# Layer 0's mixing-gate modulation: partial sums on TensorE in four column groups instead of on VectorE

## The chip, the core and the metric

The kernel runs on one core of a Trainium2 chip. The metric is device time in microseconds (us) of one execution. Five engines work side by side, each on its own queue in order: PE (TensorE, the matrix unit; the profile lists its weight loads apart as PEld), DVE (VectorE), ACT (ScalarE), POOL (GpSimd) and SP (SyncE), which here issues all the DMAs. Tiles live in SBUF; matrix products land in PSUM, in banks of 512 fp32 columns on 128 partitions.

## What is computed

A two-layer decoder trunk on 256 tokens of width 2048, in fp32. Each layer first turns a conditioning vector c into six modulation vectors of 2048 numbers, by a product with a weight matrix of 2048 x 12288:

```python
c_act = jax.nn.silu(c)
for l in range(DEPTH):                                   # DEPTH = 2
    mod = (c_act @ w_mod[l] + b_mod[l])[:, None, :]
    shift_a, scale_a, gate_a, shift_m, scale_m, gate_m = jnp.split(mod, 6, axis=-1)
    h = modulate(rms_norm(x, g_pre_mix[l]), shift_a, scale_a)
    y = hybrid_mixer(h, positions, w_in[l], ...)         # MoBA, NSA and FoX heads, then @ w_out
    x = x + gate_a * rms_norm(y, g_post_mix[l])
    h = modulate(rms_norm(x, g_pre_mlp[l]), shift_m, scale_m)
    x = x + gate_m * rms_norm(sq_relu_mlp(h, w_up[l], w_down[l]), g_post_mlp[l])
```

The six vectors are called modulation groups 0 to 5. Group 2 is gate_a, the mixing gate. For layer 0 it is needed when the product with w_out[0] leaves PSUM.

## The kernel before

**The big products.** Every weight matrix is streamed from HBM in units of 512 rows x 512 columns (1 MB, tile `raw`, [128, 4, 512]). `unit` (L225) loads one, and for each half of it ACT rounds to fp32r (`hi`, L241) and DVE takes the rest (`lo`, L242). PE then multiplies with three fp32r products (L259 to L261, `gemm_b`) or two (L287 and L289, `chunk_a`). `raw` comes from a pool of four buffers (`rawp`), `hi` and `lo` from pools of four each, so about two units are converted ahead of PE.

**The modulation.** `mod_chunk` (L119) makes part of one group. It is a generator: at each `yield` one step of 1 MB of w_mod is done. Such a step is called by `tick` after a unit of a big product or a head of attention (a `Spread` sets how many steps go to how many ticks), so the steps lie between the units. The weights come into `rawm`, from the same four buffers as `raw`, or in turn into one larger buffer (`S3` in this stretch). The step has two forms:

- On DVE: the tile is [128, 2, 1024], and for each of its two slices DVE does acc += raw * cact, with cact a number for each partition (L149 for the first slice of a chunk, L151 for the others). A chunk of 1024 columns takes 8 steps.
- On PE (`pe=True`): the tile is [128, 4, 512]. Four matmuls, one for each slice, put cact, spread to 32 columns, against the slice; each writes 32 of the 128 partitions of one PSUM tile `pm`. ACT copies `pm` to acc in the first step of a chunk (L153), DVE adds it to acc in the others (L155). A chunk of 512 columns takes 4 steps.

```python
acc = wk.tile([128, w], F32, tag="acc" if w == 1024 else "bb", name="acc", bufs=1)   # L121
...
T.matmul(pm[32 * k:32 * k + 32], cs.to_broadcast([128, 32]), raw[:, k], start=True, stop=True,
         tile_position=(0, 32 * k))                                                  # L142
...
bb = wk.tile([128, 512], F32, tag="bb", name="bb", bufs=1)                           # L165
dma(bb, ...)                                                                         # L168, bias
dma(gb, ...)                                                                         # L169, gain
T.matmul(ps, ones, acc[:, i * 512:(i + 1) * 512], start=True, stop=True)             # L171
V.scalar_tensor_tensor(bb, ps, part, bb, op0=OP.mult, op1=OP.add)                    # L172
V.scalar_tensor_tensor(gg[:, ci:ci + 512], bb, D ** 0.5, gb, op0=OP.mult, op1=OP.mult)  # L173
```

At the end of a chunk the 128 partitions of acc are summed by a matmul with ones. For a gate this is L171, once for each 512 columns; DVE then adds the bias (L172) and multiplies by the gain (L173) into `gg`. Tiles with one tag share the tag's buffers: `acc` of a 512-column chunk and `bb` have the tag "bb", which has one buffer; `acc` of a 1024-column chunk has a buffer of its own.

PSUM tiles named `pst` (`ps_t`, L68) come from two banks. They serve `pm`, the sums of L171, and in the attention heads the transposes (L463, L721) and the outputs (`po`: L726, L469, L470). `pss` (scores, L439 to L445) has two banks, `psg` (big products) four.

**Where the group lies.** In layer 0 the generator `rest` runs groups 4, 2 and 3 in this order (`G0`, L33, L585). The forms on PE are used only for groups 1 and 0 at the start (`mod_first`, L565). In the profile, group 2's steps run from 336 to 424 us: first beside the NSA heads (L718 to L732) and the first four FoX heads (`fox_attn(0)`, L763), then beside `fox_group(1)` (L645), which makes q and k of the last four heads with eight weight units. A scheduler orders each engine's instructions within the dependencies, so that an engine's order is not just the order of the code.

Of the kernel before, what the change touches and what calls it, by code (L numbers as in the profile page):

```python
# [32 lines left out]
G0 = ((0, 4), (0, 2), (0, 3))  # L33
# [12 lines left out]
def trunk(ctx, tc, x, c, positions, w_mod, b_mod, g_pre_mix, g_post_mix, g_pre_mlp, g_post_mlp, w_in, b_forget,  # L46
# [137 lines left out]
                V.scalar_tensor_tensor(m, m, 1.0, gpre[l][g // 3][:, cols], op0=OP.add, op1=OP.mult)  # L184
        yield

    def mod_groups(*lg):
        for l, g in lg:
            for q in range(2):
                yield from mod_chunk(l, g, q, 1024)  # L190

    class Spread:
        def __init__(self, gen, units, over):
# [356 lines left out]
    for l in range(DEPTH):  # L550
# [3 lines left out]
        if l == 0:  # L554
# [14 lines left out]
            def rotate(q, c0, w, parts):  # L569
# [4 lines left out]
                for t in range(2):  # L574
                    s0 = 0
                    for dst in parts:
# [5 lines left out]
                        else:  # L582
                            V.tensor_tensor(d, pw, d, OP.add)

            rest = mod_groups(*G0)  # L585

            def mod_both(q):
                for i, _ in enumerate(mod_first(q)):
# [38 lines left out]
        else:  # L627
            h, act = nxt
            ring[0] = RA
            spread[0] = Spread(mod_groups(*G1), 32, R1)  # L630

        oT = [big(TS["o"][0], [128, 8, 2, 256])]
# [173 lines left out]
        if l == 0:  # L806
            spread[0] = Spread(mod_groups((1, 1), (1, 0), (1, 4), (0, 5)), 64, MA)
        else:
            spread[0] = Spread(mod_groups((1, 5)), 16, MB)
# [131 lines left out]
```

## Time and profile before

| | us |
|---|---|
| median of 3 runs | 2440.83 (2439.29 to 2443.04) |
| the profiled execution | 2435.61 |
| its span, first to last instruction | 2433.8 |
| PE busy in the span | 2364.5 (97%) |
| DVE busy | 1641.5 (67%) |
| ACT busy | 1202.5 (49%) |

In a row of a timeline stand the start, the duration, engine, line, operation, tiles and shapes, and in brackets the idle time just before, with what ended it. Matmuls are pipelined, so the time a matmul takes from PE is read from the start of one to the start of the next, not from its duration. An fp32 matmul appears as two instructions (x2 in a row).

### The profile page before, as it was taken

What the parts mean: (1) busy time and instruction counts of PE and PEld (TensorE: products, weight loads), DVE (VectorE), ACT (ScalarE), POOL (GpSimd) and SP (SyncE); (2) the same over time, 40 slices, a digit from 0 to 9 for tenths busy, and PEclk for the clock granted to TensorE, in tenths of its full rate; (3) what the DMA queues carried; (4) which work ended last, traced back from release to release, by engine and by line L of the source; (5) the groups of instructions that cost most, each with busy time, mean ns of one, the idle gap of its engine ahead of it and who ended that gap; (6) DMA issues with size and microseconds to landing.
All of it is one profiled execution on the core that took longest, in us unless ns stands there. A gap on an engine that the chain in (4) does not pass through costs nothing.

```text
span 2433.8 us, 31894 instructions
## 1 busy us (share of the span) xinstructions
PE 2364.5 (97%) x12396; PEld 1964.0 (81%) x12396; DVE 1641.5 (67%) x2247; ACT 1202.5 (49%) x2001; POOL 12.5 (1%) x20
## 2 busy tenths in 40 slices
PE   5999999999999999999999999999999999999998
PEld 2678778778888888888877879888888888888887
DVE  3458678878777777777568467765755665655555
ACT  3434444455545535535545455554654553553553
POOL 0000000000000000000000000000000000000000
PEclk8999999999999999999999999999999999999999
DMA  9788988988888888888657688865666667666653
GB/s 356 285 326 298 307 300 288 351 303 292 279 310 278 309 296 286 303 283 308 202 184 280 209 282 303 282 231 186 222 225 225 225 231 231 219 203 199 189 190 121
DMA packets 292120, 632.82 MB, mean 260 GB/s; under 512 B 10609, under 2 KB 44801, under 8 KB 291713
## 3 DMA queue, kind: packets, MB, share of 16 engines
q1 hardware_dynamic: 291968, 630.79, 75.5%
q8 instruction: 97, 1.59, 0.3%
q14 instruction: 55, 0.44, 0.0%
HBM read 628.65 MB, written 2.10 MB: 259 GB/s over the span
## 4 chain that ended last, share of the span: by engine, by line
PE 90%; DVE 4%; DMA 3%; ACT 1%; issue 1%; POOL 0%; SPq 0%; DVEq 0%; POOLq 0%; ACTq 0%
PE psg L287 16%; PE psg L260 15%; PE psg L259 15%; PE psg L261 15%; PE psg L289 8%; PE psu L287 6%; PE psu L289 3%; PE psr L260 2%; PE psr L259 2%; PE psr L261 1%; PE pst L142 1%; PE pst L180 1%; DMA raw<-in_w_in_dram 1%; DMA S<-in_w_mod_dram 1%; DVE lo L242 1%; PE pst L340 1%
## 5 line engine op out<-in xcount | busy, mean ns | idle before, releaser
L242 DVE TENSOR_TENSOR lo<-raw,hi 128x1024 fp32r<-128x1024 f32 (+2 forms) x768 | 908.3, 1190 | 540.4 <-ACT hi L241 539.1
L241 ACT CAST hi<-raw 128x1024 fp32r<-128x1024 f32 (+2 forms) x768 | 781.7, 1025 | 900.3 <-PE psg L261 444.1
L259 PE MATMUL psg<-hi,S 128*128 128x512 f32 (+2 forms) x1664 | 639.8, 386 | 2.3 <-DVE S L354 1.2
L287 PE MATMUL psg<-S,hi 128*128 128x512 f32 x1792 | 640.1, 398 | 1.5 <-DVE lu L437 0.6
L260 PE MATMUL psg<-lo,S 128*128 128x512 f32 (+2 forms) x1664 | 638.0, 383 | 2.0 <-DVE lo L242 2.0
L261 PE MATMUL psg<-hi,S 128*128 128x512 f32 (+2 forms) x1664 | 636.8, 383 | 0.9 <-DVE S L355 0.9
L289 PE MATMUL psg<-S,lo 128*128 128x256 f32 x1792 | 500.8, 281 | 0.9 <-DVE lo L242 0.9
L287 PEld LDWEIGHTS psg<-S,hi 128*128 128x128 f32 x1792 | 336.9, 188 | 83.1 <-ACT hi L241 2.0
L259 PEld LDWEIGHTS psg<-hi,S 128*128 128x128 f32 x1664 | 312.1, 188 | 68.1 <-issue 4.5
L260 PEld LDWEIGHTS psg<-lo,S 128*128 128x128 f32 x1664 | 312.8, 188 | 62.1 <-DVE lo L242 3.6
L261 PEld LDWEIGHTS psg<-hi,S 128*128 128x128 f32 x1664 | 312.6, 188 | 61.4 <-DVE S L355 2.6
L289 PEld LDWEIGHTS psg<-S,lo 128*128 128x128 f32 x1792 | 338.3, 189 | 3.6 <-DVE lo L242 1.8
L151 DVE SCALAR_TENSOR_TENSOR acc<-rawm,cact,acc 128x1024 f32<-128x1024 f32 x226 | 289.3, 1280 | 26.6 <-DMA rawm<-in_w_mod_dram 24.9
L287 PE MATMUL psu<-S,hi 128*128 128x512 f32 x640 | 232.9, 398 | 0.0
L289 PE MATMUL psu<-S,lo 128*128 128x256 f32 x640 | 179.0, 280 | 0.0
L287 PEld LDWEIGHTS psu<-S,hi 128*128 128x128 f32 x640 | 120.2, 188 | 29.4 <-DVE xu L840 0.3
L289 PEld LDWEIGHTS psu<-S,lo 128*128 128x128 f32 x640 | 120.7, 189 | 0.3 <-issue 0.2
L260 PE MATMUL psr<-lo,S 128*128 128x512 f32 (+1 forms) x192 | 69.8, 363 | 1.5 <-DVE lo L242 1.5
L259 PE MATMUL psr<-hi,S 128*128 128x512 f32 (+1 forms) x192 | 68.8, 366 | 0.8 <-ACT hi L241 0.8
L261 PE MATMUL psr<-hi,S 128*128 128x512 f32 (+1 forms) x192 | 69.0, 359 | 0.0
L841 ACT ACTIVATE xu<-xu 128x256 f32<-128x256 f32 x120 | 49.3, 412 | 25.9 <-DVE xu L840 25.9
L151 DVE SCALAR_TENSOR_TENSOR acc<-X,cact,acc 128x1024 f32<-128x1024 f32 x48 | 61.4, 1280 | 0.3
(207 smaller groups left out, 1652.7 us busy)
## 6 DMA issues: line engine op xcount, KB each, us to landing
raw<-in_w_up_dram SPq DMA_DIRECT2D x128, 1024.0 KB, 5.4
raw<-in_w_down_dram SPq DMA_DIRECT2D x128, 1024.0 KB, 5.3
rawm<-in_w_mod_dram SPq DMA_DIRECT2D x119, 1024.0 KB, 6.6
raw<-in_w_in_dram SPq DMA_DIRECT2D x72, 1024.0 KB, 7.2
S<-in_w_mod_dram SPq DMA_DIRECT2D x16, 2048.0 KB, 11.1
raw<-in_w_out_dram SPq DMA_DIRECT2D x32, 1024.0 KB, 6.4
X<-in_w_mod_dram SPq DMA_DIRECT2D x26, 1024.0 KB, 7.5
raw<-in_w_in_dram SPq DMA_DIRECT2D x24, 688.0 KB, 5.5
```

Source lines behind the costliest of these rows:

```text
L142: T.matmul(pm[32 * k:32 * k + 32], cs.to_broadcast([128, 32]), raw[:, k], start=True, stop=True, tile_position=(0, 32 * k))
L151: V.scalar_tensor_tensor(acc, raw[:, k], cs, acc, op0=OP.mult, op1=OP.add)
L180: T.matmul(ps[:, j:j + 1], acc[:, j * 128:(j + 1) * 128], ones[:, 0:1], start=True, stop=True)
L241: A.copy(hi[:, :, :w], r)
L242: V.tensor_tensor(lo[:, :, :w], r, f32(hi[:, :, :w]), OP.subtract)
L259: T.matmul(ps[t][:, :w], xh, hi, start=first, stop=False)
L260: T.matmul(ps[t][:, :w], xh, lo, start=False, stop=False)
L261: T.matmul(ps[t][:, :w], xl, hi, start=False, stop=last)
L287: T.matmul(ps[d], hi[:, kk, ws], a.rearrange("p s n -> p (s n)"), start=(u == 0 and h == 0 and kk == 0), stop=False)
L289: T.matmul(ps[d][:, :256], lo[:, kk, ws], a[:, 0], start=False, stop=last)
L340: T.matmul(tp[:, j * 128:(j + 1) * 128], xt[:, t, k * 128:(k + 1) * 128], r, start=True, stop=True)
L841: A.activation(u, u, AF.Relu)
```

## The change

Group 2 of layer 0 is made in the form on PE. `mod_groups` gets an argument `pe` that names the groups, and cuts such a group into four chunks of 512 columns instead of two of 1024. The number of steps (16) and the bytes of each (1 MB) stay. `mod_chunk` itself is not changed. Lines behind L190 are numbered up to four higher afterwards (L463 becomes L467).

```diff
-    def mod_groups(*lg):
+    def mod_groups(*lg, pe=()):
         for l, g in lg:
-            for q in range(2):
-                yield from mod_chunk(l, g, q, 1024)
+            if g in pe:
+                for q in range(4):
+                    yield from mod_chunk(l, g, q, 512, pe=True)
+            else:
+                for q in range(2):
+                    yield from mod_chunk(l, g, q, 1024)
...
-            rest = mod_groups(*G0)
+            rest = mod_groups(*G0, pe=(2,))
```

**Order on PE, in the heads.** Before, around the two sums of the first chunk (L171), among heads and the first products of `fox_group(1)`; numbers behind a tile's name tell one buffer's use from the next:

```order
L469 MATMUL pst_3078<-PT_3076,X4_160 128x256
L470 MATMUL pst_3078<-PT_3076,X4_160 128x128
L171 MATMUL pst_3092<-acc_2726,cst_82 128x512
L441 MATMUL pss_3140<-cst_82,lu_3141 128x128
L442 MATMUL pss_3140<-X1_2279 128x256
L444 MATMUL pss_3140<-cst_82,lf_151 128x128
L445 MATMUL pss_3140<-cst_82,lu_3141 128x256
L171 MATMUL pst_3100<-acc_2726,cst_82 128x512
L463 MATMUL pst_3124<-cst_82,P_3113 128x128
```

Now, from the fourth step of the first chunk to the next use of its sum's bank:

```order
L142 MATMUL pst_2894<-rawm_2892,cact_92 32x512 x4
L445 MATMUL pss_3059<-cst_82,lu_3060 128x128
...
L171 MATMUL pst_2905<-acc_2726,cst_82 128x512
L725 MATMUL pst_2909<-cst_82,pc_2756 15x128 x2
L449 MATMUL pss_3059<-cst_82,lu_3060 128x256
L467 MATMUL pst_2929<-cst_82,P_2917 128x128 x3
L730 MATMUL pst_2935<-pcT_2912,vcmp_2517 128x256
...
L449 MATMUL pss_3090<-cst_82,lu_3091 128x256
L467 MATMUL pst_2954<-cst_82,P_2942 128x128 x3
```

The steps stand between heads as sets of four matmuls (L142), and the sum of a chunk follows shortly behind its fourth step, while heads are still to come; `pst_2954` is the next tile that takes the bank of `pst_2905`.

**Order on SP, the DMAs of the same stretch.** Before, the bias and gain of the first chunk stand early, and the first two weight units of `fox_group(1)` (L227) follow:

```order
L133 DMA S3_2939<-in_w_mod_dram 128x2x1024
L168 DMA bb_3088<-in_b_mod_dram 128x512
L169 DMA gb_3089<-in_g_post_mix_dram 128x512
L133 DMA rawm_3136<-in_w_mod_dram 128x2x1024
L133 DMA S3_3002<-in_w_mod_dram 128x2x1024
L133 DMA rawm_3171<-in_w_mod_dram 128x2x1024
L227 DMA raw_3180<-in_w_in_dram 128x4x512
...
L227 DMA raw_3222<-in_w_in_dram 128x4x512
```

Now:

```order
L133 DMA rawm_3169<-in_w_mod_dram 128x4x512
L133 DMA S3_2965<-in_w_mod_dram 128x4x512
L133 DMA rawm_3208<-in_w_mod_dram 128x4x512
L168 DMA bb_2901<-in_b_mod_dram 128x512
L169 DMA gb_3130<-in_g_post_mix_dram 128x512
L133 DMA S3_3036<-in_w_mod_dram 128x4x512
L231 DMA raw_3221<-in_w_in_dram 128x4x512
L231 DMA raw_3263<-in_w_in_dram 128x4x512
L168 DMA bb_3129<-in_b_mod_dram 128x512
```

The bias of a chunk (`bb`) waits for the buffer that its `acc` holds until L171 has read it, and loads of w_mod stand ahead of it. The first unit of weights, `raw_3221`, takes the buffer of `rawm_3003`, which PE reads in the second chunk's second step.

## Rows read from the trace of the kernel before

**Rows 1.** The page, part 1: busy time, share of the span, instructions, by engine.

```profile
PE 2364.5 (97%) x12396; PEld 1964.0 (81%) x12396; DVE 1641.5 (67%) x2247; ACT 1202.5 (49%) x2001; POOL 12.5 (1%) x20
```

**Rows 2.** Windows: stretch, length, busy PE, PEld, DVE, ACT, POOL, clock, DMA, GB/s.

```profile
336.00:424.00 88.00, 81.74 (x452) 65.81 (x451) 79.63 (x168) 46.31 (x116) 0.00 (x0) 1.00 0.82 290
...
427.00:440.00 13.00, 9.45 (x51) 7.42 (x52) 12.25 (x35) 6.70 (x20) 0.00 (x0) 1.00 1.00 391
```

**Rows 3.** Windows of L151 alone: stretch, length, busy DVE.

```profile
336.00:424.00 88.00, 38.27 (x30) 1.00 0.82 290
```

**Rows 4.** Waits of PE, 336 to 427 us: total, times, longest.

```profile
PE pss L439 <- DVE mx L451: 2.2, 3, 1.0
PE psg L289 <- DVE lo L242: 0.9, 1, 0.9
PE pst L463 <- DVE S L474: 0.8, 1, 0.8
```

**Rows 5.** Timeline of PE around one step of groups 1 and 0.

```profile
105.71 0.39 PE L261 MATMUL psg<-hi,S 128*128 128x512 f32 x1
106.02 1.06 PE L142 MATMUL pst<-S,cact 128*32 128x512 f32 x8
107.02 0.50 PE L259 MATMUL psg<-hi,S 128*128 128x512 f32 x1
107.35 0.39 PE L260 MATMUL psg<-lo,S 128*128 128x512 f32 x1
```

**Rows 6.** Timeline of PE: one sum over partitions (L171) and what follows.

```profile
374.35 1.02 PE L171 MATMUL pst<-acc,cst 128*128 128x512 f32 x2
375.21 0.38 PE L441 MATMUL pss<-cst,lu 128*128 128x128 f32 x2
```

**Rows 7.** DVE's adds of L155 (duration min/median/max), then PE behind a chunk's last step.

```profile
L155 DVE TENSOR_TENSOR acc<-pst,acc x24: 684/692/693, 18.0 to 186.4; 128x512 f32<-128x512 f32 x24
...
80.82 1.05 PE L180 MATMUL pst<-cst,acc 128*128 128x1 f32 x8 [0.81 <-DVE acc L155]
```

**Rows 8.** Timelines: sum on PE, bias load on SP, its use on DVE; landing of `bb`.

```profile
417.75 1.88 PE L171 MATMUL pst<-acc,cst 128*128 128x512 f32 x4
...
420.25 0.34 SPq L168 DMA_DIRECT2D bb<-in_b_mod_dram  x1
...
423.56 0.69 DVE L172 SCALAR_TENSOR_TENSOR bb<-pst,bb 128x512 f32<-128x512 f32 x1 [0.40 <-DMA bb<-in_b_mod_dram]
...
DMA to landing us min/median/max: 3.2/4.5/7.7
```

**Rows 9.** Timeline of PE in a FoX head.

```profile
366.13 0.60 PE L442 MATMUL pss<-X 128*128 128x256 f32 x2
366.56 0.38 PE L444 MATMUL pss<-cst,lf 128*128 128x128 f32 x2
366.78 0.60 PE L445 MATMUL pss<-cst,lu 128*128 128x256 f32 x2
367.22 0.59 PE L469 MATMUL pst<-PT,X 128*128 128x256 f32 x2
367.65 0.38 PE L470 MATMUL pst<-PT,X 128*128 128x128 f32 x2
```

**Rows 10.** Timeline of PE in `fox_group(1)`: one pair of its products.

```profile
397.99 0.40 PE L287 MATMUL psg<-S,hi 128*128 128x512 f32 x1
...
398.34 0.40 PE L287 MATMUL psg<-S,hi 128*128 128x512 f32 x1
```

**Rows 11.** DMA issues (count, KB, median us to landing), and ACT's cast of half a unit.

```profile
raw<-in_w_in_dram SPq DMA_DIRECT2D x72, 1024.0 KB, 7.2
...
367.86 1.05 ACT L241 CAST hi<-raw 128x1024 fp32r<-128x1024 f32 x1
```

**Rows 12.** PE behind a long wait, and the granted clock (1.00 is full) after it.

```profile
283.16 0.62 PE L522 MATMUL pst<-cst,hp 128*128 128x15 f32 x4 [2.29 <-ACT hp L519]
...
284.00:286.00 2.00, 1.77 (x4) 1.30 (x5) 1.90 (x7) 1.26 (x3) 0.00 (x0) 0.50 1.04 379
```

## The prediction

> **What bounds the kernel now.** The page's first part comes first: PE is busy for 97% of the span, DVE for 67% [rows 1]. So on average PE time added is paid in full, and DVE time saved is worth only the waits of PE that it ends. But the group lies in one stretch, and the windows have to say whether that average holds there. From 336 to 424 us PE is busy for 81.74 of 88 us and DVE for 79.63 [rows 2]: this is the one kind of place where DVE is nearly as full as PE. 38.27 us of DVE's time there are the group's own 30 accumulations [rows 3]. PE stands idle for 88 - 81.74 = 6.26 us. The waits of PE name the reasons: the three longest that DVE ends are 2.2 us (row maxima of the heads), 0.9 us (`lo` of a weight unit) and 0.8 us (an output tile) [rows 4]. From 427 to 440 us, in the last four heads, it idles for another 13 - 9.45 = 3.55 us [rows 2], but there DVE works on group 3, which doesn't change. So the change relieves a crowded DVE in a place where that crowding costs PE at most 6.26 us.
>
> **The change, part by part.**
>
> *Added on PE: 16 steps.* The start of the kernel already runs this form between big products, so its price is read there: the product before a step starts at 105.71, the two after it at 107.02 and 107.35 [rows 5]. Without the step the two would follow at PE's pace, which is 0.23 us a product (107.02 less 105.71 would be 0.23, and 107.35 less 107.02 too). So a step costs 107.35 - 105.71 - 2 x 0.23 = 1.18 us of PE. The pace of 0.23 is an estimate from rows of half the size: in `fox_group(1)` a 512-column and a 256-column product together take 398.34 - 397.99 = 0.35 us [rows 10], two thirds of which is 0.23. 16 steps are 16 x 1.18 = 18.9 us. All of it lies in PE's queue; what it can hide in are waits of PE, which are counted below. For a floor I take the steps' rows alone, 107.02 - 106.02 = 1.00 us, or 16.0 us.
>
> The four column groups do overlap in that row: the eight instructions take 1.0 us, where one full-width fp32 matmul of the same 512 columns, the sum of L171, takes 375.21 - 374.35 = 0.86 us alone [rows 6].
>
> *Removed from DVE, and what comes back.* 30 accumulations (38.27 us) and two first slices go; 12 adds from PSUM at 0.69 us come, 8.3 us [rows 3, 7], and ACT gets four copies. DVE so gets some 30 us of room in 88 us. It can give PE back at most the 6.26 us of idle time, and nothing if other waits take their place. I take the three named waits, 2.2 + 0.9 + 0.8 = 3.9 us [rows 4]. What is late next is the softmax's own way through DVE, ACT and PE.
>
> *Added: a bias that can't be loaded early.* Now `acc` of a chunk and `bb` share one buffer. So the load of the bias waits until L171 has read acc, and L172 waits for the load. Meanwhile L171's PSUM tile holds one of the two `pst` banks, which the heads need, and DVE stands in its queue at L172. The profile before has this chain once: L171 at 417.75, load issued at 420.25, L172 at 423.56 for 0.69 us, 6.5 us in all [rows 8]. By its parts it is 0.86 for one sum [rows 6], 3.2 to 7.7 for the landing [rows 8] and 0.69: 4.75 to 9.25 us.
>
> How much of this PE covers is read off its new order. First chunk: from L171 to the next tile in its bank stand L171 itself (0.86), five matmuls of 0.43 and five of 0.22 [rows 9], and three transposes (0.33, as three halves of 0.22): 4.4 us. So PE waits for 0.3 to 4.8 us; I take 1.5. Second chunk: its bank, or its place in DVE's queue, is wanted after L171, three transposes, one head's output and ten products of `fox_group(1)`, 0.86 + 0.33 + 0.65 + 10 x 0.175 = 3.6 us [rows 6, 9, 10]; that leaves 1.1 to 5.6, and I take 2.5. Third chunk: some sixty products (10 us) follow before the bank is wanted; nothing. Fourth: 24 products (4.2 us) and a head's scores, then the row maxima of the last heads stand behind L172 on DVE; 0 to 3.5, I take 1. Sum 5 us, bounds 1.4 to 13.9. On SP the first chunk's next gain load waits for L173, and the first weight unit of `fox_group(1)` stands behind it; that unit has to wait longer for its own buffer (next), so this costs nothing more.
>
> *Moved: weight buffers that PE holds.* Before, DVE freed a `rawm` buffer as soon as it had added it up. Now it is held until PE comes to the step. The first weight unit of `fox_group(1)` goes into the buffer of the second chunk's second step. From that step on a load takes 7.2 us and the cast 1.05 [rows 11], 8.25 us; PE has until the unit's first product about 5.4 us of work (ten matmuls of heads by [rows 9], nine transposes, one step). So it is late by some 2.8 us, less what PE has already waited on the way: I take 2. The second unit is covered by most of the first one's products, two steps and a sum, 8 us or more. Bounds 0 to 5.7. Later units alternate with steps; two units ahead are converted, which covers one load. The loads keep their 1 MB.
>
> *Added: one PSUM round per step.* DVE's add takes 0.69 us, and PE behind the last step of a chunk waited 0.81 us for it where nothing stood between [rows 7]. In the heads the bank of a step is soon wanted again, with two or three matmuls (0.65 to 0.87 us) between; beside the weight units there is room enough. Eight steps and one sum are exposed, up to 0.81 us each: 0 to 7.3, and I take 1.5.
>
> The Trainium skill speaks against the change at this place: "TensorEngine Tiling (Array Packing)", section "PSUM Bottleneck", says that tiling makes TensorE faster but not the emptying of PSUM, so that the copy may become the bottleneck. By that rule each of the 16 steps would wait for its evacuation, and the sum would end near the upper bound instead. [Rows 7] shows the wait once a chunk, not once a step; the matmuls between decide.
>
> *The sum.* 18.9 - 3.9 + 5 + 2 + 1.5 = +23.5 us. On the profiled execution (2435.6) that gives 2459; it ran 5.2 us below the median of the runs shown, 2440.8, so the forecast for a median is 2464. The rest of the kernel keeps its order up to small moves and is bound by PE, so nothing after the stretch takes the time back.
>
> **The rivals.**
>
> *PE's price alone.* DVE's room also shortens the waits of the new chains, and the steps fill the gaps: 16.0 to 18.9 less up to 6.3, with new waits of 0 to 3. That is +10 to +15, a time of about 2453. For it: DVE's queue would be half empty, and the scheduler has put the steps between heads. Against it: the bias chain is a DMA and no engine's room shortens it.
>
> *The bias chain and PSUM decide.* Each chunk stops PE by the longer landing time, and steps wait for their banks: 18.9 + 13.9 + 5.7 + 3 with nothing back, +35 to +42, about 2479. For it: three loads of 1 MB stand ahead of the first bias in SP's order. Waits this long bring a second price: after a wait of 2.29 us the granted clock read 0.50, the lower level of 1.2 GHz, for the next stretch [rows 12], where every product takes twice as long; one such drop adds 1 to 2 us.
>
> *The other side: DVE was the bound.* If in this crowded stretch DVE set the pace throughout, and PE's busy time only hid it, the steps would run in time that PE loses anyway. It is decided by the price of a step: to be faster by 0.2% (4.9 us, about what a measurement of this kernel can tell from no change), all 6.26 + 3.55 = 9.8 us of waits [rows 2] would have to go and the 16 steps cost less than 0.3 us each, a quarter of what the row shows. It would give about 2433. DVE's 79.63 of 88 us speak for it; PE's 81.74 against.
>
> *Not four abreast.* If beside the heads the column groups ran one after another, a step would cost four times 0.86 us [rows 6], 55 us in all, about 2495. The order shows the same sets of four as at the start, so I see no reason.
>
> **How the numbers follow.** Forecast (+15 to +32): 0.58. PE's price alone (+5 to +15): 0.17. The chain decides (+32 to +45): 0.13. No change within 4.9 us: 0.05. Faster: 0.04. Not four abreast: 0.03. The predicted time is the forecast's, 2464. The range from 2452 to 2482 (+11 to +41) holds the forecast, somewhat over half of the second case and most of the third, about 0.8. Faster by over 0.2%: 0.04; within 0.2%: 0.05; slower: 0.91.
>
> **What would show it.** In the profile after, L142 should have 16 more steps, starts 1.0 us apart from first to next product, and the stretch of the group should be some 20 to 25 us longer with DVE's busy share down from nine tenths to about six. The waits of PE should name DVE's `bb` or `pst` behind L171, and `hi` at the first unit of `fox_group(1)`; the row maxima's 2.2 us should be gone or smaller. After the stretch, stages should be equally long. The prediction is wrong if PE's idle time in the stretch falls by more than the steps add, if a step costs less than 0.9 us between heads, or if the bias lands late enough to stop all four chunks.

## The result and the profile after

The changed kernel takes 2455.8 us (median), the kernel before 2441.4 us beside it: the ratio is 1.0058, with a 95% interval of 1.0040 to 1.0075, so it is slower by some 14 us (10 to 18). The forecast was 2464 us, 23.5 us more; the time lies inside the range from 2452 to 2482, near its lower end.

The page's first part of the changed kernel shows what moved (engine, busy us, share of the span, instructions):

```profile
PE 2387.5 (97%) x12524; PEld 1970.3 (80%) x12524; DVE 1615.8 (66%) x2227; ACT 1205.6 (49%) x2005; POOL 12.5 (1%) x20
```

Against [rows 1], PE has 128 matmuls and 23 us more, DVE 26 us less. PE's share stays at 97%, because the span grew with it.

To see where the time went, the same work must be measured in both. I use **the long stretch**: from the first compressed head (or the step of L142 right ahead of it) to the first product of the boundary behind `w_out` (L340, now L344). It is cut once more at the first head of `fox_attn(1)`. The end of the heads alone is no good mark, because products of `w_out` stand between the last heads and their number differs from kernel to kernel. Windows of the kernel before (stretch; length, then busy PE, PEld, DVE, ACT, POOL with instruction counts; granted clock, DMA share, GB/s):

```profile
341.35:427.14 85.79, 78.71 (x434) 62.99 (x431) 76.81 (x162) 46.32 (x116) 0.00 (x0) 1.00 0.85 303
427.14:534.92 107.78, 103.55 (x485) 84.86 (x485) 88.99 (x118) 51.64 (x90) 1.10 (x2) 1.00 0.92 335
341.35:534.92 193.57, 182.26 (x919) 147.85 (x916) 165.79 (x279) 97.96 (x206) 1.10 (x2) 1.00 0.89 321
```

The same of the changed kernel:

```profile
344.88:446.22 101.34, 97.28 (x561) 65.80 (x561) 55.60 (x145) 49.26 (x120) 0.00 (x0) 1.00 0.77 261
446.22:553.24 107.02, 102.69 (x486) 84.51 (x485) 88.00 (x119) 51.85 (x90) 1.09 (x2) 1.00 0.91 328
344.88:553.24 208.36, 199.98 (x1045) 150.31 (x1045) 143.59 (x263) 101.11 (x210) 1.09 (x2) 1.00 0.84 295
```

The long stretch grows by 208.36 - 193.57 = 14.8 us, all of it in the first part, which answers [rows 2]. PE's busy time grows by 199.98 - 182.26 = 17.7 us, and its idle time falls from 193.57 - 182.26 = 11.3 to 8.4 us, by 2.9. So 17.7 - 2.9 = 14.8; the medians differ by 2455.8 - 2441.4 = 14.4. The two profiled executions differ by 2455.1 - 2433.8 = 21.3 us of span. Of the other 6.5 us, 3.5 arose before the stretch, which starts at 344.88 in place of 341.35, above all at one wait for a rounded weight (`hi`), which takes 0.67 us in the kernel before:

```profile
278.83 0.51 PE L263 MATMUL psg<-hi,S 128*128 128x268 f32 x2 [2.40 <-ACT hi L245]
```

In a second execution of the same kernel (below) the stretch starts at 341.11, so these 3.5 us don't belong to the change. The last 3.0 us arose behind the stretch; in the executions of the experiments that leave the work there as it is, that part is from 1.3 us shorter to 5.4 us longer than in the kernel before, so they say nothing of the change either.

A step between products of `fox_group(1)`, PE's timeline (start, us, what), answers [rows 5]:

```profile
402.77 0.28 PE L293 MATMUL psg<-S,lo 128*128 128x256 f32 x1
402.98 1.06 PE L142 MATMUL pst<-rawm,cact 128*32 128x512 f32 x8
403.97 0.50 PE L291 MATMUL psg<-S,hi 128*128 128x512 f32 x1
404.31 0.28 PE L293 MATMUL psg<-S,lo 128*128 128x256 f32 x1
```

The step holds PE for 403.97 - 402.98 = 0.99 us, and about 0.1 us more goes at each edge: from 402.77 to 404.31 are 1.54 us, less the 0.35 that this pair of products takes without a step [rows 10], which leaves 1.19 us. The steps among the heads read the same within 0.1 us. 16 such steps are 19.0 us, but PE's busy time grows by 17.7, 1.11 a step: it is some 1.3 us lower elsewhere in the stretch, and no run shows where.

PE's waits from 344.9 to 446.2 us (total, times, longest) answer [rows 4]:

```profile
PE pst L473 <- ACT PT L469: 1.7, 3, 0.6
PE pss L443 <- DVE mx L455: 0.7, 1, 0.7
PE pst L730 <- ACT PT L469: 0.6, 1, 0.6
PE pst L467 <- DVE bb L172: 0.4, 1, 0.4
PE pst L171 <- DVE acc L155: 0.3, 1, 0.3
```

The row maxima's 2.2 us are 0.7, and the waits for `lo` and for an output tile are gone. In part the row maxima's wait has only moved: behind this window, in `fox_attn(1)`, it grew from 1.4 to 2.3 us. What is left is mostly the softmax's own path through ACT. No unit of weights is late; the bias shows with 0.4 us here, and the PSUM round with 0.3. Behind the second chunk's sum, where the 0.4 us are, PE's timeline has these rows:

```profile
388.99 1.02 PE L171 MATMUL pst<-acc,cst 128*128 128x512 f32 x2
...
392.80 1.06 PE L142 MATMUL pst<-rawm,cact 128*32 128x512 f32 x8
394.25 0.55 PE L467 MATMUL pst<-cst,P 128*128 128x128 f32 x3 [0.39 <-DVE bb L172]
```

PE had work for 394.25 - 0.39 - 388.99 = 4.9 us before it had to wait, a step of the third chunk among it.

### The profile page after: what moved, and what is told of

The parts are those of the page before. It is cut to its first block, busy times and chain, and to the rows that moved or that the text cites. A ratio compares the mean times of both kernels' runs of the same rounds, so it can differ in the third digit from the quotient of the medians.

```text
span 2455.1 us, 32145 instructions
## 1 busy us (share of the span) xinstructions
PE 2387.5 (97%) x12524; PEld 1970.3 (80%) x12524; DVE 1615.8 (66%) x2227; ACT 1205.6 (49%) x2005; POOL 12.5 (1%) x20
## 4 chain that ended last, share of the span: by engine, by line
PE 91%; DVE 3%; DMA 3%; ACT 1%; issue 1%; POOL 0%; SPq 0%; DVEq 0%; POOLq 0%; ACTq 0%
PE psg L291 16%; PE psg L263 15%; PE psg L264 15%; PE psg L265 15%; PE psg L293 8%; PE psu L291 6%; PE psu L293 3%; PE pst L142 2%; PE psr L264 2%; PE psr L263 1%; PE psr L265 1%; PE pst L180 1%; DVE lo L246 1%; DMA S<-in_w_mod_dram 1%; DMA rawm<-in_w_mod_dram 1%; PE pst L344 1%
## 5 line engine op out<-in xcount | busy, mean ns | idle before, releaser
L151 DVE SCALAR_TENSOR_TENSOR acc<-rawm,cact,acc 128x1024 f32<-128x1024 f32 x203 | 259.9, 1280 | 22.1 <-DMA rawm<-in_w_mod_dram 20.3
L155 DVE TENSOR_TENSOR acc<-pst,acc 128x512 f32<-128x512 f32 x36 | 24.9, 691 | 58.5 <-PE pst L142 49.4
## 6 DMA issues: line engine op xcount, KB each, us to landing
S<-in_w_mod_dram SPq DMA_DIRECT2D x16, 2048.0 KB, 11.3
```

The costliest lines, as they stand in the source:

```text
L151: V.scalar_tensor_tensor(acc, raw[:, k], cs, acc, op0=OP.mult, op1=OP.add)
L155: V.tensor_tensor(acc, pm, acc, OP.add)
```

## The experiments

Three questions were open behind this ledger: whether PE's new work is really paid in full, whether the 2.9 us that came back are owed to DVE's relief, and what the bias and the smaller chunks would cost by themselves. Most experiments show their long stretch as one window row (length, then PE's busy time as the first two numbers). The us behind a ratio are worked out on 2440 us.

**PE's work without DVE's relief.** On the kernel before:

```
-            if pe:
+            if pe or (l, g) == (0, 2):
                 pm = ps_t()
...
                 cs = cact[:, kn * u + k:kn * u + k + 1]
+                [T.matmul(pm[32 * j:32 * j + 32], cs.to_broadcast([128, 32]), raw[:, k, 512 * (j % 2):512 * (j % 2) + 512],
+                          start=True, stop=True, tile_position=(0, 32 * j)) for j in (2 * k, 2 * k + 1) if (l, g) == (0, 2)]
```

> The kernel before, in which PE also does the four column-tiled matmuls of each of the 16 load units of group 2 into a PSUM tile that nobody reads, while DVE keeps all its accumulations and chunks, buffers and biases are as before. This is the added PE work without any of DVE's relief. Theory (16 x 1.16 us, paid in full; DVE's relief gives 3 us back in the changed kernel): 17 to 20 us slower than before, the stretch 103 to 106 us. Rival (what shrank PE's waits in the changed kernel is that PE itself takes longer, not that DVE has room): 13 to 16 us slower, as the changed kernel, the stretch 99 to 102 us.

The ratio is 1.0057 (1.0043 to 1.0071), +13.9 us. The long stretch:

```profile
342.02:550.43 208.41, 202.26 (x1046) 151.83 (x1046) 168.02 (x279) 97.65 (x206) 1.09 (x2) 0.99 0.82 291
```

208.4 us, as in the changed kernel, although DVE keeps all its work (168.02 us busy). Some 1.7 us of it (8 x 0.21) are owed to a lower granted clock, which the changed kernel's first execution doesn't have there:

```profile
525.00:533.00 8.00, 7.18 (x29) 5.60 (x29) 5.15 (x6) 3.51 (x4) 0.00 (x0) 0.79 1.00 343
```

PE's idle time is 208.41 - 202.26 = 6.2 us, 5.2 less than before. The rival holds: PE's waits shrink because PE itself comes later to what it waits for, not because DVE has room.

**DVE's relief without PE's work.** On the kernel before:

```
-  V.scalar_tensor_tensor(acc, raw[:, k], cs, acc, op0=OP.mult, op1=OP.add)
+  n = 256 if (l, g) == (0, 2) else w
+  V.scalar_tensor_tensor(acc[:, :n], raw[:, k, :n], cs, acc[:, :n], op0=OP.mult, op1=OP.add)
```

This kernel leaves out three quarters of each accumulation.

> The kernel before, in which each of the 30 accumulations of layer 0's group 2 takes 256 of the 1024 columns (the rest of the sum is left out); PE gets no new work. This shows what DVE's room alone gives back. Theory (DVE's crowding costs PE the three named waits, 2.2 + 0.9 + 0.8): 2 to 4 us faster than before, the stretch of 85.8 us comes to 82 to 84 us. Rival (DVE's room is worth all of PE's idle time): 5 to 7 us faster, 79 to 81 us. Rival (the waits only change their names): within 1 us.

The ratio is 0.9993 (0.9985 to 1.0002), -1.7 us and not to be told from nothing. The long stretch:

```profile
340.90:534.51 193.61, 184.08 (x918) 149.63 (x916) 146.39 (x279) 97.63 (x206) 1.09 (x2) 0.98 0.87 319
```

DVE has 19 us less to do, and PE's idle time falls by 1.8 us, to 9.5. In this execution PE's busy time rose by as much: in `fox_attn(1)` it waited 2.64 us for the row maxima, as PE's timeline shows,

```profile
429.51 0.46 PE L439 MATMUL pss<-X 128*128 128x128 f32 x2 [2.64 <-DVE mx L451]
```

and the window behind it has the clock at 0.53:

```profile
430.00:432.00 2.00, 2.00 (x8) 1.60 (x7) 2.00 (x3) 1.52 (x6) 0.00 (x0) 0.53 1.00 396
```

The first theory (2 to 4 us) is at most just met: the interval reaches from 3.7 us faster to 0.5 slower. Relieving the crowded DVE is worth some 2 us.

**Each step twice.** On the changed kernel:

```
-                if pe:
+                for _ in range(2 if pe and g == 2 else 1 if pe else 0):
                     T.matmul(pm[32 * k:32 * k + 32], ...)
```

> The changed kernel with each of the 16 steps' four matmuls issued twice, nothing else. This measures what a set of four costs PE where it stands. Theory (a step's price is PE time that is paid in full, 1.0 us for a set between other work): the stretch from the first compressed head to the first head of fox_attn(1) grows from 101.3 us by 16 x 1.0 = 16 us less at most 2 us of PE's 4 us of idle time, so 115 to 118 us; the kernel is 14 to 17 us longer than the changed one, +28 to +32 against the kernel before. Rival (in the changed kernel the steps stand partly in time that PE would wait anyway): the second set hides as well, +5 to +12 us over the changed kernel.

The ratio is 1.0084 (1.0070 to 1.0098), +20.5 us. A step on PE's timeline:

```profile
350.57 1.94 PE L142 MATMUL pst<-rawm,cact 128*32 128x512 f32 x16
352.45 0.39 PE L725 MATMUL pst<-cst,pc 128*15 128x128 f32 x2
```

and the long stretch:

```profile
341.18:559.28 218.10, 213.18 (x1174) 155.10 (x1174) 144.12 (x263) 101.11 (x210) 1.10 (x2) 1.00 0.78 277
```

The loop stands inside that over the slices, so each of the four matmuls follows itself. The eight take 352.45 - 350.57 = 1.88 us, so the second four cost 0.89, not 1.0. PE's busy time is 13.2 us above the changed kernel's and its idle time 3.5 us below (4.9), +9.7 us. The theory (+14 to +17 us) misses. The rival's time (+5 to +12) is met by the stretch, its reason only in part: the second matmuls are paid for the most part, but PE's remaining waits still give way. By the medians it is 3 to 6 us above the two runs of the changed kernel, with an uncertainty of some 5.

**The bias in a buffer of its own.** On the changed kernel:

```
-        acc = wk.tile([128, w], F32, tag="acc" if w == 1024 else "bb", name="acc", bufs=1)
+        acc = wk.tile([128, 1024 if gate else w], F32, tag="acc" if w == 1024 or gate else "bb", name="acc", bufs=1)[:, 0:w]
```

`gate`, set ahead of this line, is true for groups 2 and 5.

> The changed kernel, but acc of the four chunks has the buffer of the wide acc, so the bias no longer shares it and can be loaded early. Theory after the trace (the chain over the bias costs PE 0.4 us where 5 us were predicted, as the heads and weight units that stand behind it cover it): no change against the changed kernel, -1 to +1 us, the stretch 100 to 102 us. Rival (the chain costs what was predicted, and the trace only shows it under other names): 4 to 6 us shorter, the stretch 95 to 97 us.

The ratio is 1.0041 (1.0027 to 1.0054), +10.0 us. The long stretch:

```profile
341.63:548.48 206.85, 200.27 (x1045) 150.53 (x1045) 143.84 (x263) 100.15 (x210) 1.10 (x2) 1.00 0.84 296
```

It is 1.5 us shorter than the changed kernel's, with 6.6 us of idle time in place of 8.4. By the medians the gain is 4 us against the first run of the changed kernel and 7 against the second, with an uncertainty of some 5. The first part of the stretch is 99.8 us, just under the theory's 100 to 102 and above the rival's 95 to 97. So the chain costs more than the 0.4 us that PE's wait for `bb` names; the rest stands under other names. Up to the first head of `fox_attn(1)` PE idles for 2.9 us in place of 4.1, and behind it for 3.7 in place of 4.3.

**The changed kernel again.**

> The changed kernel once more, unaltered, to see what of its differences belongs to the stretch and what to a single execution. Expected: +13 to +17 us against the kernel before, and 207.5 to 209.5 us from the first compressed head to the boundary (208.4 in the first profile), while the time ahead of the stretch and behind it moves by some 3 us either way.

The ratio is 1.0070 (1.0054 to 1.0086), +17.1 us. The long stretch:

```profile
341.11:552.43 211.32, 202.35 (x1045) 152.58 (x1045) 143.63 (x263) 101.09 (x210) 1.09 (x2) 0.98 0.83 291
```

It is 3 us longer than in the first execution, outside of what I expected. Its waits have 1.6 us for `bb` in place of 0.4, but its idle time is only 0.6 us longer (8.97); the other 2.4 us are busy time, and the clock fell twice, neither time behind a wait for the bias (last section). So the two executions lie 1.5 and 4.5 us above the kernel with the bias apart; of the 4.5, some 2 us are waits, and that the chain brought on the drops of the clock is not shown.

**The small chunks on DVE, with the shared bias and without.** The first takes only the chunks from the change, the second adds the edit of `acc` above:

```
                 for q in range(4):
-                    yield from mod_chunk(l, g, q, 512, pe=True)
+                    yield from mod_chunk(l, g, q, 512)
```

> The change without its PE part: group 2 of layer 0 goes in four chunks of 512 columns, summed by DVE as before (64 accumulations of half the width), so that the smaller chunks and the bias that shares acc's buffer stand alone. Measured from the first compressed head to the first product of the boundary behind w_out, 193.6 us in the kernel before and 208.4 us in the changed one. Theory (PE's 16 steps are the whole loss, and the own buffer for the bias was worth 1.5 us): 193 to 196 us, the kernel within 2 us of before. Rival (the chain over the bias costs 5 us or more once DVE is as crowded as before): 198 to 205 us, 4 to 11 us slower.

> The four chunks of 512 columns on DVE again, but acc in the wide buffer, so that the bias no longer shares it: the small chunks without the chain over the bias. From the first compressed head to the boundary's first product the kernel before took 193.6 us, the four chunks on DVE with the shared buffer 213.9 us. Theory (DVE, in whose queue L172 stands waiting for the bias, is what made the small chunks on DVE slow; PE's relief of DVE hides that chain in the changed kernel): 194 to 200 us, the kernel 0 to 6 us slower than before. Rival (64 accumulations of 0.75 us in place of 32 of 1.28 us, 7 us more on a full DVE, are the cause): 208 us or more, 12 us or more slower.

With the shared buffer the ratio is 1.0060 (1.0043 to 1.0076), +14.6 us, as slow as the change itself, without any step of group 2 on PE. The long stretch:

```profile
341.11:554.98 213.87, 191.79 (x916) 154.18 (x914) 172.29 (x308) 98.32 (x206) 1.10 (x2) 0.95 0.82 290
```

DVE's timeline at the start of `fox_group(1)`:

```profile
388.94 0.69 DVE L172 SCALAR_TENSOR_TENSOR bb<-pst,bb 128x512 f32<-128x512 f32 x1 [4.36 <-DMA bb<-in_b_mod_dram]
389.55 1.22 DVE L246 TENSOR_TENSOR lo<-raw,hi 128x1024 fp32r<-128x1024 f32 x1
```

and PE's:

```profile
390.82 0.39 PE L293 MATMUL psg<-S,lo 128*128 128x256 f32 x1 [2.92 <-DVE lo L246]
```

DVE stands at L172 for 4.36 us until the bias has landed; the `lo` of a weight unit is queued behind it, and PE waits 2.92 us for that. The delay comes round a second time: `lo` also frees the buffer of a later weight unit. Its second half ends at 393.23, that unit's load is issued at 393.25, and PE waits for its `hi`; rows of DVE, SP, ACT and PE:

```profile
392.01 1.22 DVE L246 TENSOR_TENSOR lo<-raw,hi 128x1024 fp32r<-128x1024 f32 x1
393.25 0.37 SPq L231 DMA_DIRECT2D raw<-in_w_in_dram  x1
398.44 1.99 ACT L245 CAST hi<-raw 128x1024 fp32r<-128x1024 f32 x2 [10.41 <-DMA raw<-in_w_in_dram]
399.54 1.22 PE L291 MATMUL psg<-S,hi 128*128 128x512 f32 x2 [3.77 <-ACT hi L245]
```

Over the long stretch PE waits 7.2 us for `hi` and 6.2 for `lo` in `fox_group(1)`; with the bias apart (next) it is 1.3 and 2.8. PE's idle time is 22.1 us, and with the clock at 0.95 its busy time is 9.5 us above before. Both expectations of this kernel missed; the loss is larger than the rival's. With the bias apart the ratio is 1.0020 (1.0010 to 1.0031), +4.9 us:

```profile
341.38:538.89 197.51, 184.50 (x918) 149.07 (x916) 171.38 (x309) 98.36 (x206) 1.10 (x2) 0.99 0.88 315
```

213.87 - 197.51 = 16.4 us are the chain's price on a crowded DVE in these two executions, 7.3 of them busy time, for the most part at the lower clock; by the ratios it is 9.7 us, with an uncertainty of some 5. The theory holds. In the changed kernel the same chain costs 1.5 to 4.5 us by the traces and 4 to 7 by the ratios, so only the traces tell the two apart. In the changed kernel `lo` stands right behind L172 as well; DVE's timeline:

```profile
393.51 0.69 DVE L172 SCALAR_TENSOR_TENSOR bb<-pst,bb 128x512 f32<-128x512 f32 x1 [0.81 <-DMA bb<-in_b_mod_dram]
394.12 1.22 DVE L246 TENSOR_TENSOR lo<-raw,hi 128x1024 fp32r<-128x1024 f32 x1
```

The bias landed sooner there, but that isn't all: behind the third chunk DVE stood at L172 for 2.09 us with the chunks on DVE and for 1.90 in the changed kernel's second execution, and PE waited 2.52 us for `lo` in the one and not at all in the other. So the chain that the change itself brings is hidden in the changed kernel. That DVE's relief hides it is argued: PE also comes later there, and no run separates the two.

**A shorter addition from PSUM.** On the changed kernel, in group 2, with most of each addition left out:

```
-  V.tensor_tensor(acc, pm, acc, OP.add)
+  n = 64 if g == 2 else w; V.tensor_tensor(acc[:, :n], pm[:, :n], acc[:, :n], OP.add)
```

> The changed kernel, in which DVE's 12 additions from PSUM take 64 of the 512 columns (the rest of these sums is left out), so that a step's PSUM tile is emptied early and DVE is relieved once more. Theory (the matmuls between the steps cover the emptying): the same stretch, 208.4 us, comes to 207.5 to 209 us, the kernel within 2 us of the changed one. Rival (the emptying of PSUM sets the pace of the steps): 3 to 7 us shorter, 201 to 205 us.

The ratio is 1.0066 (1.0049 to 1.0082), +16.1 us, no faster than the changed kernel. The long stretch, 2 us above the expected one, with the clock at 0.98 and PE's busy time 2.0 us above the changed kernel's:

```profile
339.79:551.12 211.33, 202.00 (x1045) 152.65 (x1045) 137.94 (x263) 101.25 (x210) 1.10 (x2) 0.98 0.82 291
```

Emptying PSUM doesn't set the pace of the steps.

**Half of the change.** Two chunks on PE, then one of 1024 columns on DVE:

```
-                for q in range(4):
-                    yield from mod_chunk(l, g, q, 512, pe=True)
+                for q, w in ((0, 512), (1, 512), (1, 1024)):
+                    yield from mod_chunk(l, g, q, w, pe=w == 512)
```

> Half of the change: the first two chunks of group 2 go to PE in column groups (8 steps), the second half of the group is one chunk of 1024 columns on DVE as before. Theory (a step costs 1.1 us of PE time that is paid in full, and PE's waits shrink a little because PE itself is later): 8 x 1.1 less 1 to 3, +6 to +8 us; 199.5 to 202 us from the first compressed head to the boundary, against 193.6 and 208.4. Rival (the first steps are nearly free, as DVE's relief is worth most where DVE is fullest): +0 to +4 us, 193.5 to 197.5 us.

The ratio is 1.0023 (1.0013 to 1.0034), +5.6 us; the long stretch is +3.6 us:

```profile
342.82:540.02 197.20, 190.80 (x981) 150.26 (x981) 158.13 (x273) 99.23 (x208) 1.10 (x2) 0.99 0.86 312
```

The ratio lies between the theory and the rival, the stretch inside the rival's range. PE works 8.5 us more and idles 4.9 us less (6.4). Some of the 8.5 us is a drop of the clock, so it isn't the price of eight steps:

```profile
367.00:370.00 3.00, 3.00 (x12) 2.44 (x11) 1.45 (x5) 0.00 (x0) 0.00 (x0) 0.50 0.81 298
```

The first eight steps take back about 5 us of PE's waits, as much as sixteen do without the chain over the bias (6.2 us of idle time with the steps added, 6.6 with the bias apart). The second eight, at 14.8 - 3.6 = 11.2 us (8.6 by the ratios), take back nothing, and with the chain the idle time rises again to 8.4.

**The other way round.** If a step costs PE 1.1 us, moving the steps of the first groups from PE to DVE should win. In the kernel before, both groups went to DVE in the second to fourth quarter:

```
-  yield from mod_chunk(0, g, q, 512, pe=g in PES, tags=(("S2", 2), ("S3", 2)))
+  yield from mod_chunk(0, g, q, 512, pe=g in PES and q == 0, tags=(("S2", 2), ("S3", 2)))
```

and in another kernel one of them:

```
+  yield from mod_chunk(0, g, q, 512, pe=g in PES and (q == 0 or g == 1), tags=(("S2", 2), ("S3", 2)))
```

> The change turned round on the kernel before: the two modulation groups that PE sums at the start go to DVE in the second to fourth quarter (24 steps of PE fewer, 96 accumulations of 512 columns more on DVE, 18 additions fewer). Theory (a step costs PE 1.1 us wherever PE is full, and it was full there: 99 of 101 us): at least the 16 steps of the last two quarters come back, less what DVE, with 32 + 20 of 53 us in a quarter then nearly full, makes PE wait: 8 to 18 us faster than before. Rival (the loads set the pace there, with the transfers at 0.87 already): 0 to 5 us faster. Rival (the sums end late, and the norm of the next quarter waits for DVE): up to 15 us slower.

> As the kernel with both first groups on DVE, but only one of them (the shift, group 0) goes to DVE in the second to fourth quarter: 12 steps of PE fewer. Theory (a step costs PE 1.1 us, paid in full): 8 of the 12 steps lie where PE is full, 9 to 13 us faster than before; DVE has room (32 + 8 of some 48 us). Rival (the loads set the pace): 0 to 4 us faster. Rival (the norm waits for DVE): slower.

Both are slower: 1.0057 (1.0041 to 1.0073) and 1.0074 (1.0058 to 1.0090). My theory missed by some 22 us or more, twice. The rival in which the norm waits for DVE has the time right, but the wait is another. PE's longest group of waits from 40 to 335 us, of the kernel with both (1.5 us in the kernel before):

```profile
PE psr L260 <- DVE lo L242: 19.8, 8, 4.7
```

One such place, DVE's timeline:

```profile
136.31 2.32 DVE L151 SCALAR_TENSOR_TENSOR acc<-S,cact,acc 128x512 f32<-128x512 f32 x3
138.55 2.35 DVE L242 TENSOR_TENSOR lo<-raw,hi 128x1024 fp32r<-128x1024 f32 x2
```

and PE's:

```profile
139.82 0.78 PE L260 MATMUL psr<-lo,S 128*128 128x512 f32 x1 [2.87 <-DVE lo L242]
```

Three accumulations stand ahead of the `lo` that PE waits for. DVE isn't full: from 120 to 140 us it is busy for 15 of 20 us. It is late at the moment that counts, and there the clock falls too:

```profile
120.00:140.00 20.00, 13.00 (x49) 9.85 (x49) 15.00 (x22) 5.52 (x6) 0.00 (x0) 0.83 0.80 296
```

With one group it is the same wait, 11.5 us in five places, and 5.8 us for `hi`; why that kernel is no faster than the one with both is not shown. A share of busy time, 32 of 53 us, was the wrong measure for room.

**A version that beats both.** The kernel before has the chain over bias and gain too [rows 8]. Loading the bias straight into `gg`, and the second gain into the buffer that comes free, takes it away:

```
-  bb = wk.tile([128, 512], F32, tag="bb", name="bb", bufs=1)
-  gb = wk.tile([128, 512], F32, tag="gb", name="gb", bufs=1)
+  gb = wk.tile([128, 512], F32, tag=("gb", "bb")[i], name="gb", bufs=1)
   ci = q * w + i * 512
+  bb = gg[:, ci:ci + 512]
```

> The kernel before, whose group stays on DVE, but the bias is loaded straight into its part of gg and the second gain has a buffer of its own, in all four mixing and MLP gates, so that no bias or gain waits for another's buffer. The first two experiments on the small chunks showed what such a chain costs on a crowded DVE (16 us for four chunks); the kernel before has it in the second half of each of its two chunks. Theory (it costs there too, though less): 1 to 4 us faster than before, 190 to 193 us from the first compressed head to the boundary in place of 193.6. Rival (with chunks of 1024 columns nothing urgent stands behind the bias on DVE): within 1 us. Rival (the earlier small loads hold back the weights in the load queue): up to 3 us slower.

The ratio is 0.9986 (0.9977 to 0.9995), 3.4 us faster than before, as the theory has it. The profile doesn't say where: the long stretch is no shorter in the profiled execution.

```profile
340.75:534.58 193.83, 184.88 (x919) 149.36 (x917) 166.56 (x279) 98.46 (x206) 1.10 (x2) 0.98 0.88 320
```

PE idles for 8.95 us there in place of 11.3, but a drop of the clock cost 2.6 us of busy time. The edit also touches the three other gates. That the chain was the cause is argued, not shown.

## Why the forecast was right in its sign and 6 to 9 us too long

- **The bound** held: PE was full, and its added work showed up in the span. With PE's work alone (DVE's kept) the loss is 14.8 us, some 1.7 of it a drop of the clock; with the bias apart the changed kernel's stretch loses 206.85 - 193.57 = 13.3.
- **The price of a step** was 1.18 us, 18.9 in all; read the same way it measured 1.19. The floor of 1.00 was the bare set; each edge costs 0.1. PE's busy time grew by 17.7 us only, 1.2 less than the term, and where PE saved this is open.
- **Waits that come back**, -3.9 us: without the chain they are 11.3 - 6.6 = 4.7 us, so the size was near. The reason was wrong. I gave them to DVE's room; DVE's room alone takes 1.8 us of PE's idle time away, PE's steps alone 5.2. The rival "DVE was the bound" falls with it.
- **The bias chain**, +5 us, bounds 1.4 to 13.9: 1.5 and some 2 us by the traces of two executions, 4 to 7 by the ratios with an uncertainty of some 5. The first chunk was covered, PE's wait behind the second was 0.4 and 1.6 us where I took 2.5, and the fourth made PE wait no longer in `fox_attn(1)` than before (4.3 us of idle time behind its first head, 4.2 before). What was mis-sized is what PE covers, behind the second chunk above all: it had work for 4.9 us where I counted 3.6. I also let the landing time alone decide: on a crowded DVE the same chain cost 16.4 us in one pair of executions, above my upper bound (9.7 by the ratios, within it). And the 6.5 us that I read in the profile before [rows 8] are not this chain: there the load at 420.25 waits for L173 of the half before, which ends at 420.22, and not for L171.
- **Weight buffers that PE holds**, +2 us: nothing; no wait for `hi` stands among PE's waits in this part.
- **A PSUM round per step**, +1.5 us: 0.3 us, and a shorter addition gains nothing. The rule of the Trainium skill that I weighed against the change ("TensorEngine Tiling (Array Packing)", section "PSUM Bottleneck") doesn't bite in this kernel, where other products stand between the steps.
- **The sum.** From 23.5 to 14.8: 1.2 of PE's busy time, 0.8 of the waits, 3.2 of the chain (5 for 1.8 us of idle time), 2 of the weights and 1.5 of the PSUM rounds, 8.7 together. All five differences have one sign, so no luck hid an error. The rival "PE's price alone" (+10 to +15, 2453) has the first measurement, 14 us; the second, 17, lies in the lower end of my own range. Its reason, that DVE's room shortens the new chains, is argued, as said above.
- Not four abreast: no; the eight instructions of a step take 0.99 us. Behind the stretch the time differs by 3.0 us, within what single executions differ by there.

## What to carry to other kernels

Work moved from an engine that is busy for two thirds of the span to one that is busy for 97% of it is paid for nearly in full, here 14.8 us for 17.7 of work; the waits that shrink on the way shrink for the most part because the full engine comes later, and here the first half of the move used up nearly all of them. Moving it back isn't free either: in a queue kept in order, what counts is which urgent instruction stands behind the new work, not the engine's share of busy time. And when a chunk's shape changes, look at which small loads now share a buffer: the same wait for a bias cost 16 us on a crowded queue in one pair of executions (some 10 by the ratios) and 1.5 to 4.5 on a relieved one.

## What the runs showed of the hardware that I had not expected

**The clock does not fall behind every long wait, and it falls behind some short ones.** At the same place, the changed kernel's first execution waited 2.27 us (PE's timeline):

```profile
450.41 0.46 PE L443 MATMUL pss<-X 128*128 128x128 f32 x2 [2.27 <-DVE mx L455]
```

and the clock stayed at full speed in the window behind it:

```profile
450.00:454.00 4.00, 2.65 (x14) 1.80 (x15) 4.00 (x15) 2.43 (x8) 0.00 (x0) 1.00 1.04 388
```

The second waited 2.31 us:

```profile
447.55 0.77 PE L443 MATMUL pss<-X 128*128 128x128 f32 x2 [2.31 <-DVE mx L455]
```

and most of the 4 us around and behind it ran at the lower level, 1.2 GHz:

```profile
447.00:451.00 4.00, 3.45 (x13) 2.94 (x13) 3.51 (x10) 1.79 (x6) 0.00 (x0) 0.57 1.04 392
```

The second execution's clock fell once more, behind a wait of 0.82 us:

```profile
529.61 0.79 PE L264 MATMUL psg<-lo,S 128*128 128x512 f32 x1 [0.82 <-DVE lo L246]
...
529.00:533.00 4.00, 3.39 (x9) 2.73 (x10) 3.96 (x4) 0.21 (x1) 0.00 (x0) 0.57 0.79 245
```

The first waited 0.8 us for the same `lo`, and its clock stayed at 1.00. PE's busy time in the long stretch differs by 202.35 - 199.98 = 2.4 us between the two. [Rows 12] showed such a drop behind 2.29 us. So the length of the wait just before doesn't tell whether the clock falls.

**Half as wide is not half as long on DVE.** The accumulation over 512 columns takes 0.75 us where 1024 columns take 1.28, so 64 of the one are 48 us and 32 of the other 41. DVE's groups in the small chunks on DVE (count, busy us, mean ns):

```profile
L151 DVE SCALAR_TENSOR_TENSOR acc<-rawm,cact,acc 128x512 f32<-128x512 f32 x43 | 32.1, 746 | 0.9 <-DMA rawm<-in_w_mod_dram 0.2
L151 DVE SCALAR_TENSOR_TENSOR acc<-rawm,cact,acc 128x1024 f32<-128x1024 f32 x2 | 2.6, 1279 | 0.0
```

**Column-group matmuls issued twice are cheaper the second time:** the four take 0.99 us, and the eight, each behind itself, 1.88, so 0.89 for the second four.
